# First gather one expert at a time, and a last expert with a plain one-hot, high and low parts, single blocks and a separate output buffer

## The chip, the cores and the metric

The kernel runs on one core of a Trainium2 chip. The metric is the time of one execution on the device in microseconds (us); shown are the median of several runs and one execution taken by the hardware profiler. TensorE is called PE (its weight loads PEld), VectorE V or DVE, ScalarE A or ACT, GpSimd G or POOL, and SyncE SP; SP issues the weight loads.

## The reference, cut to what matters

One transformer layer over 512 latent tokens with 1024 channels. The mixer (attention, Hyena, Fourier) comes first and isn't touched by the change. Then comes a mixture of 16 experts in which each expert chooses its 64 tokens, and a final norm:

```python
x = x + g1 * yx
h2 = modulate(rms_norm(x, norm2_g[l]), sh2, sc2)
x = x + g2 * expert_choice_moe(h2, w_router[l], w_gate[l], w_up[l], w_down[l])
return rms_norm(x, final_g)

def expert_choice_moe(h, w_router, w_gate, w_up, w_down):
    cap = CAPACITY_FACTOR * n // N_EXPERTS                  # 64
    aff = jax.nn.softmax(jnp.einsum('bld,de->ble', h, w_router), axis=-1)
    top_w, top_i = lax.top_k(aff.transpose(0, 2, 1), cap)
    xg = jax.vmap(lambda hb, ib: hb[ib])(h, top_i)
    a = jnp.einsum('becd,edf->becf', xg, w_gate)
    u = jnp.einsum('becd,edf->becf', xg, w_up)
    y = jnp.einsum('becf,efd->becd', jax.nn.silu(a) * u, w_down) * top_w[..., None]
    return scatter_add(y, top_i)                            # back to the tokens
```

Every expert has three weights of 8 MB in float32 (1024 x 2048 twice, 2048 x 1024), so 16 of them are some 400 MB that have to be read.

## The kernel before, in words

**The weights.** All expert weights form one stream of blocks of 1 MB (128 partitions x 2048 numbers): for each expert 8 blocks of wg, 8 of wu and 8 of wd. The last expert's wd is stored apart (`wdl`), in the order of the column blocks of `LASTD` (line 183): each entry has its first column, its width and how many of the 16 row blocks (fb) lie in each piece. `loads` (line 1101) gives the buffers in a fixed rotation: raw tiles that hold two blocks (T2b, T2a, T3a, T1_0, T1_1, wsp, T3b) and single `ld` buffers. The trace writes T1_0 and T1_1 both as rawT. `prefetch` (line 1116) issues the next load on SP's queue; where a raw tile takes the two halves of one pair of blocks, one load of 2 MB brings both (line 1129). SP's queue is in order: a load waits there until PE has read what was in the buffer. When the experts begin, 22 blocks have already been loaded.

**The gather.** Tokens are picked by matmul. `onehot` (line 1354) writes, for 128 tokens and one expert, which token goes to which of 64 places (`iota` equal to `slot`), times a value per token: rs4, the inverse norm, for the gather. `gather(pr)` (line 1362) does it for a pair of experts: eight one-hots, those of the second expert's last two token tiles on G, and then for each of 8 channel blocks k four matmuls into PSUM (gx), with x1 as weights and the one-hots of both experts as 128 moving columns. V and A move gx to xg with the norm's scale and shift. The pair's gather runs as a generator inside `up` of the expert ahead; for pair 0 it runs inside `up(0)` itself, one k ahead of each block of weights.

**An expert.** `up(e)` (line 1387) multiplies xg with wg (pa) and wu (pu), 4 matmuls of 512 columns a block, in pairs that fill the two halves of the array's columns; then silu, product (hid), transposition (hp, hidT). `down` (line 1431) multiplies with wd (py) and scales by g2b. `scatter_map` (line 1447) builds a one-hot with the affinity as value, transposes it (stp) to st, and after each pair 8 matmuls (sc) put the results back onto the tokens, where V adds them to acc. The order of the instructions on each engine is set by a scheduler, as far as data allow, from the order in which the code is written.

**The last expert** (lines 1491 to 1549). Its one-hot stands twice in st, because py keeps even and odd fb apart in two halves of the partitions and the scatter adds them. The columns are done in the four blocks of LASTD: py, V's multiply by g2b (Yq), four sc matmuls of full float32 in `finish` (line 1499), V's addition to x1, squares on A with their sums in ms16, and G's multiply of x1 by the final gain in place. `order` keeps PE's sequence of these as written; finish of a block comes after the first weight piece of the next. Then the mean of the squares, a root on A and a Newton step on V give r, x1 is scaled by it, and five stores write the output.

Of the kernel before, what the change touches and what calls it, by code (L numbers as in the profile page):

```python
# [182 lines left out]
LASTD = (0, 256, (8, 8)), (256, 256, (8, 8)), (512, 384, (4, 4, 4, 4)), (896, 128, (8, 8))  # L183
# [9 lines left out]
def _body(tc, nc, es, a, out, dbg, stop):  # L193
# [1253 lines left out]
    def scatter_map(pr, es2=(0, 1)):  # L1447

        for h_, e2 in enumerate(es2):
            onehot(oh, pr, e2, lambda t, e: aff[:, t, e:e + 1], h_)  # L1450
# [3 lines left out]
        st = M["mo"].tile([128, 512], F32, name="st")  # L1454
# [37 lines left out]
    st = scatter_map(7, (1, 1))  # L1492
# [3 lines left out]
    Yq = mo.tile([128, 1024], F32, name="Yq", tag="Y2")  # L1496
    order = tc.keep_in_program_order

    def finish(q):
# [15 lines left out]
        for t in range(0, 4, 2):  # L1515
            G.tensor_mul(x1[:, t:t + 2, qs], x1[:, t:t + 2, qs], fgb[:, None, qs].to_broadcast([128, 2, w]))
# [3 lines left out]
    for q, (c0, w, fbs) in enumerate(LASTD):  # L1520
# [11 lines left out]
        V.tensor_mul(Yq[:, qs], o[:, :w], M["g2b"][:, qs])  # L1532
    finish(len(LASTD) - 1)

    ms, s_, r = (mo.tile([128, 4], F32, name=n) for n in ("msf", "sf", "rf"))
    V.tensor_reduce(ms, ms16, axis=AX.X, op=OP.add)
    V.tensor_scalar(ms, ms, 1.0 / D, EPS, op0=OP.mult, op1=OP.add)
# [31 lines left out]
```

## Time and profile before

| what | us |
|---|---|
| median of three runs | 1476.78 |
| the three runs | 1473.26, 1477.72, 1476.78 |
| the profiled execution | 1474.33 |
| its span, first to last instruction | 1472.5 |
| PE busy, share of the span | 1354.8 (92%) |
| DVE, ACT, POOL busy | 495.1, 287.7, 114.8 |
| mean granted PE clock | 0.986 |

The profile's page says PE 48% and DMA 42% for the chain of work that ended last. Up to some 470 us the mixer runs; the route (norm, router, top 64) ends at 538 us; the experts take from there to 1464 us; scaling and storing the output take the rest. In the 40 slices of the page, DMA moves 382 to 396 GB/s from 552 to 663 us and 419 to 432 GB/s from there to 1436 us.

### The profile page before, as it was taken

What the parts mean: (1) busy time and instruction counts of PE and PEld (TensorE: products, weight loads), DVE (VectorE), ACT (ScalarE), POOL (GpSimd) and SP (SyncE); (2) the same over time, 40 slices, a digit from 0 to 9 for tenths busy, and PEclk for the clock granted to TensorE, in tenths of its full rate; (3) what the DMA queues carried; (4) which work ended last, traced back from release to release, by engine and by line L of the source; (5) the groups of instructions that cost most, each with busy time, mean ns of one, the idle gap of its engine ahead of it and who ended that gap; (6) DMA issues with size and microseconds to landing.
All of it is one profiled execution on the core that took longest, in us unless ns stands there. A gap on an engine that the chain in (4) does not pass through costs nothing.

```text
span 1472.5 us, 16253 instructions
## 1 busy us (share of the span) xinstructions
PE 1354.8 (92%) x6659; PEld 712.1 (48%) x6659; DVE 495.1 (34%) x984; ACT 287.7 (20%) x513; POOL 114.8 (8%) x141
## 2 busy tenths in 40 slices
PE   5899999999999989999999998988989988988996
PEld 2667668777788953433434333322423422423323
DVE  5676687665546551030121121120101101201123
ACT  5554225444334210000000000000000000000003
POOL 2133431000100100000000000000000000000002
PEclk9899999999999999999999999999999999999998
DMA  9424786111445489999999999999999999999994
GB/s 379 182 77 154 286 279 151 64 47 41 145 155 203 147 345 382 391 396 419 430 428 428 431 425 432 424 430 427 431 427 426 431 425 431 425 429 429 429 428 194
DMA packets 62037, 478.69 MB, mean 325 GB/s; under 512 B 6781, under 2 KB 11519, under 8 KB 17930
## 3 DMA queue, kind: packets, MB, share of 16 engines
q1 hardware_dynamic: 57384, 464.21, 76.9%
q0 software_dynamic: 2752, 9.05, 2.4%
q10 hardware_dynamic: 1826, 4.40, 0.9%
q8 instruction: 52, 0.85, 0.2%
q14 instruction: 23, 0.19, 0.0%
HBM read 473.02 MB, written 4.21 MB: 324 GB/s over the span
## 4 chain that ended last, share of the span: by engine, by line
PE 48%; DMA 42%; DVE 5%; ACT 3%; issue 1%; POOL 1%; ACTq 0%; SPq 0%; DVEq 0%
DMA rawwsp<-in_wu_dram 6%; PE pmm L229 6%; PE pmm L230 6%; PE pmm L231 6%; PE pa L1402 6%; PE pu L1402 5%; PE py L1438 5%; DMA ld<-in_wd_dram 4%; DMA rawT2b<-in_wu_dram 4%; DMA rawT<-in_wd_dram 3%; DMA rawT3a<-in_wd_dram 3%; DMA ld<-in_wg_dram 3%; DMA rawT<-in_wu_dram 3%; PE gx L1371 2%; DMA rawT2b<-in_wg_dram 2%; DMA ld<-in_wu_dram 2%
## 5 line engine op out<-in xcount | busy, mean ns | idle before, releaser
L1416 DVE TENSOR_TENSOR hid<-hid,pu 128x512 f32<-128x512 f32 x32 | 20.7, 684 | 419.8 <-PE pu L1402 406.2
L229 PE MATMUL pmm<-T,wsp 128*128 128x512 f32 x288 | 116.3, 407 | 0.7 <-ACT T L234 0.7
L231 PE MATMUL pmm<-T,wsp 128*128 128x512 f32 x288 | 113.9, 395 | 2.2 <-DVE wsp L235 2.2
L230 PE MATMUL pmm<-T,wsp 128*128 128x512 f32 x288 | 114.2, 397 | 0.1
L1415 ACT ACTIVATE hid<-pa 128x512 f32<-128x512 f32 x32 | 17.4, 594 | 408.1 <-PE pa L1402 390.2
L1371 PEld LDWEIGHTS gx<-vt,x 128*128 128x128 f32 x512 | 61.6, 191 | 41.3 <-issue 34.9
L1371 PE MATMUL gx<-vt,x 128*128 128x128 f32 x512 | 71.7, 287 | 4.5 <-DVE vt L1356 1.9
L1444 DVE TENSOR_TENSOR Y<-py,g2b 64x512 f32<-64x512 f32 x30 | 20.7, 689 | 161.8 <-PE py L1438 147.3
L1356 POOL TENSOR_SCALAR vt<-iota,slot,rs 128x64 f32<-128x64 f32 x16 | 10.3, 670 | 737.4 <-PE stp L1453 714.1
L235 DVE TENSOR_TENSOR wsp<-ld,wsp 128x1024 fp32r<-128x1024 f32 (+1 forms) x39 | 51.5, 1330 | 45.3 <-ACT wsp L234 43.1
L229 PEld LDWEIGHTS pmm<-T,wsp 128*128 128x128 f32 x288 | 54.4, 190 | 21.4 <-issue 7.8
L231 PEld LDWEIGHTS pmm<-T,wsp 128*128 128x128 f32 x288 | 54.6, 190 | 16.2 <-DVE wsp L235 2.6
L1480 PE MATMUL sc<-Y,st 128*128 128x512 f32 (+1 forms) x128 | 57.0, 598 | 4.8 <-DVE Y L1444 4.8
L230 PEld LDWEIGHTS pmm<-T,wsp 128*128 128x128 f32 x288 | 54.7, 190 | 12.6 <-issue 1.7
L1424 ACT ACTIVATE hidT<-hp 128x512 f32<-128x512 f32 x16 | 9.6, 598 | 249.1 <-PE hp L1419 129.6
L1438 PE MATMUL py<-rawT,hidT 128*64 128x512 f32 x216 | 50.0, 600 | 4.0 <-DMA rawT<-in_wd_dram 3.9
L234 ACT ACTIVATE wsp<-ld 128x1024 fp32r<-128x1024 f32 (+1 forms) x39 | 41.8, 1078 | 54.1 <-PE pmm L230 32.8
L1484 DVE TENSOR_TENSOR acc<-acc,sc 128x512 f32<-128x512 f32 x56 | 38.1, 686 | 12.3 <-PE sc L1480 12.3
L1480 PEld LDWEIGHTS sc<-Y,st 128*128 128x128 f32 (+1 forms) x128 | 23.5, 189 | 38.6 <-issue 26.4
L1402 PE MATMUL pu<-rawT,K1n 128*64 128x512 f32 x152 | 36.6, 599 | 3.3 <-DMA rawT<-in_wu_dram 3.2
L1438 PE MATMUL py<-ld,hidT 128*64 128x512 f32 x168 | 38.9, 596 | 0.5 <-DMA ld<-in_wd_dram 0.5
L1028 DVE TENSOR_REDUCE sm<-pbig 128x1 f32<-128x768 f32 x32 | 30.5, 955 | 17.2 <-PE pbig L1026 17.1
(566 smaller groups left out, 2337.3 us busy)
## 6 DMA issues: line engine op xcount, KB each, us to landing
ld<-in_wmod_dram SPq DMA_DIRECT2D x24, 1024.0 KB, 6.4
ld<-in_wg_dram SPq DMA_DIRECT2D x24, 1024.0 KB, 22.0
ld<-in_wd_dram SPq DMA_DIRECT2D x21, 1024.0 KB, 27.0
ld<-in_wu_dram SPq DMA_DIRECT2D x21, 1024.0 KB, 22.0
rawT<-in_wu_dram SPq DMA_DIRECT2D x10, 2048.0 KB, 9.2
ld<-in_win_dram SPq DMA_DIRECT2D x19, 1024.0 KB, 6.1
rawT<-in_wg_dram SPq DMA_DIRECT2D x8, 2048.0 KB, 29.2
rawT<-in_wd_dram SPq DMA_DIRECT2D x15, 1024.0 KB, 19.6
```

Source lines behind the costliest of these rows:

```text
L229: mm(o, ah, bh, start=first, stop=False)
L230: mm(o, ah, bl, start=False, stop=False)
L231: mm(o, al, bh, start=False, stop=last)
L234: keep(A.activation(hi, src, AF.Copy))
L235: keep((eng or V).tensor_sub(lo, src, hi.bitcast(F32)))
L1028: V.tensor_reduce(sm[:, 0:1], pb[:, :768], axis=AX.X, op=OP.max)
L1371: mm(o[:, k % 4], x1[:, t, k * 128:(k + 1) * 128], oh[:, t], start=t == 0, stop=t == 3)
L1402: mm(ob[64 * hf:64 * hf + 64], xg[:, k, es_], w_[:, (2 * b + hf) * 512:(2 * b + hf + 1) * 512], start=k == 0, stop=k == 7)
L1416: V.tensor_mul(hid[:, bs], hid[:, bs], acc_[1][b] if e == NE - 1 else acc_[1][:, bs])
L1438: mm(o[64 * dh:64 * dh + 64, :], hcol(hT_, fb), w_[:, i * 1024 + dh * 512:i * 1024 + (dh + 1) * 512], start=fb == 0, stop=fb == 15)
L1480: mm(o, st[ks, t * 128:(t + 1) * 128], Y2[ks, ds_], start=True, stop=True)
L1484: V.tensor_add(acc[:, t, ds_], acc[:, t, ds_], o)
```

## The change

Five things, all in the experts' part:

- `gather0` takes the place of gather(0): expert 0 first, with its four one-hots and 64 moving columns, then expert 1 with the same. Its generator has 16 steps instead of 8, and `up(0)` takes one ahead of each of its 16 blocks. G no longer writes one-hots.
- Two pairs of blocks in the last expert's wu (stream numbers 372 to 375) are loaded singly.
- The last expert's one-hot has no value; the affinity of its 64 tokens is gathered by 4 matmuls of one column (affc) and multiplied into Yq with g2b.
- LASTD's first two blocks of 256 columns become one of 512. For all blocks but the last, Yq is split into a high and a low part (A copies, V subtracts), and the scatter is two matmuls in the one-pass format per token tile instead of one in float32.
- The multiply by the final gain goes to a buffer of its own, xo, without waiting for the squares. V does it for two token tiles of the 384-wide block and for the whole last block. Part of the mean is taken ahead, two squares of the last block are on V, and the output leaves in seven pieces instead of five.

```diff
-LASTD = (0, 256, (8, 8)), (256, 256, (8, 8)), (512, 384, (4, 4, 4, 4)), (896, 128, (8, 8))
+LASTD = (0, 512, (4, 4, 4, 4)), (512, 384, (4, 4, 4, 4)), (896, 128, (8, 8))
...
-            if len(js) == 2 and stream[j][1] == 0:
+            if len(js) == 2 and stream[j][1] == 0 and j < 24 * NE - 12:
...
+    def gather0():
+        XG[0] = xg0
+        for h in range(2):
+            hs_ = slice(h * CAP, (h + 1) * CAP)
+            onehot(oh, 0, h, lambda t, e: rs4[:, t:t + 1], h)
+            for k in range(8):
+                if k % 4 == 0:
+                    o = pmm("gx")[:, :4 * CAP].rearrange("p (k n) -> p k n", k=4)
+                for t in range(4):
+                    mm(o[:, k % 4], x1[:, t, k * 128:(k + 1) * 128], oh[:, t, hs_], start=t == 0, stop=t == 3)
...
-            onehot(oh, pr, e2, lambda t, e: rs4[:, t:t + 1], e2, lambda t: G if e2 and t >= 2 else V)
+            onehot(oh, pr, e2, lambda t, e: rs4[:, t:t + 1], e2)
...
-        gat = gather(0) if e == 0 else gather(e // 2 + 1) if e % 2 and e < NE - 1 else iter(())
+        gat = gather0() if e == 0 else gather(e // 2 + 1) if e % 2 and e < NE - 1 else iter(())
...
-    st = scatter_map(7, (1, 1))
+    onehot(oh, 7, 1, None, 0)
+    onehot(oh, 7, 1, None, 1)
...
+        mm(o[:, :1], oh[:, t], aff[:, t, NE - 1:NE], start=t == 0, stop=t == 3)
+    affc, m0 = c16[:, 0:1], c16[:, 4:8]
+    V.tensor_copy(affc, o[:, :1])
...
-                order(mm(o[:, t - t0, :w], st[:, t * 128:(t + 1) * 128], Yq[:, qs], start=True, stop=True))
+                s_ = st[:, t * 128:(t + 1) * 128]
+                if q == last:
+                    order(mm(o[:, t - t0, :w], s_.bitcast(F32), Yq[:, qs], start=True, stop=True))
+                else:
+                    for i in range(2):
+                        order(mm(o[:, t - t0, :w], s_, Yhl[:, i, qs], start=i == 0, stop=i == 1))
...
-        for t in range(0, 4, 2):
-            G.tensor_mul(x1[:, t:t + 2, qs], x1[:, t:t + 2, qs], fgb[:, None, qs].to_broadcast([128, 2, w]))
+        if q < last:
+            for t in range(0, 4, 2):
+                (V if q == last - 1 and t else G).tensor_mul(xo[:, t:t + 2, qs], x1[:, t:t + 2, qs], fgb[:, None, qs].to_broadcast([128, 2, w]))
...
-        V.tensor_mul(Yq[:, qs], o[:, :w], M["g2b"][:, qs])
+        V.scalar_tensor_tensor(Yq[:, qs], o[:, :w], affc, M["g2b"][:, qs], op0=OP.mult, op1=OP.mult)
+        if q < last:
+            split(Yq[:, qs], Yhl[:, 0, qs], Yhl[:, 1, qs])
...
+    V.tensor_tensor(xo[:, :, qs], x1[:, :, qs], fgb[:, None, qs].to_broadcast([128, 4, qs.stop - qs.start]), op=OP.mult)
...
-    for i, (t, c0, c1) in enumerate(((0, 0, 512), (1, 0, 1024), (0, 512, 1024), (2, 0, 1024), (3, 0, 1024))):
+    for e_, t, c0, c1 in ((V, 0, 0, 512), (A, 1, 0, 512), (V, 0, 512, 1024), (A, 1, 512, 1024), (V, 2, 0, 1024), (A, 3, 0, 512),
+                          (V, 3, 512, 1024)):
```

What stands on PE in the first up projection, before, from the first gather matmul on (gx the gather, pa and pu the weights' matmuls, rawT_0 is T1_0; x7 are seven in a row, each of which the profile shows as two instructions):

```order
L1371 MATMUL gx<-vt,x_3183 128x128 x7
L1402 MATMUL pa<-rawT2b,K1n 64x512 x4
L1371 MATMUL gx<-vt,x_3183 128x128 x5
L1402 MATMUL pu<-rawT_0_4221,K1n 64x512
L1402 MATMUL pa<-rawT2b,K1n 64x512 x4
L1371 MATMUL gx<-vt,x_3183 128x128 x7
L1402 MATMUL pa<-rawT2a,K1n 64x512 x4
L1371 MATMUL gx<-vt,x_3183 128x128 x5
```

Two more groups of four follow among the later weights, six in all. Now, at the same place on PE:

```order
L1376 MATMUL gx<-vt,x_3183 128x64 x14
L1423 MATMUL pa<-rawT2b,K1n 64x512 x4
L1376 MATMUL gx<-vt,x_3183 128x64 x8
L1423 MATMUL pu<-rawT_0_4221,K1n 64x512
L1423 MATMUL pa<-rawT2b,K1n 64x512 x4
L1376 MATMUL gx<-vt,x_3183 128x64 x8
L1423 MATMUL pu<-rawT_0_4221,K1n 64x512
L1423 MATMUL pa<-rawT2a,K1n 64x512 x4
L1376 MATMUL gx<-vt,x_3183 128x64 x8
```

These hold all 32 matmuls of expert 0 and 6 of expert 1; the other 26 follow in seven groups of two or four between the pu blocks, eleven groups in all.

On PE behind the last up projection, before (py the down projection of the last expert, sc the scatter):

```order
L1528 MATMUL py<-rawT3b,hidT 64x256 x16
L1528 MATMUL py<-ld,hidT 64x256 x8
L1506 MATMUL sc<-Yq,st 128x256 x4
L1528 MATMUL py<-rawT2b,hidT 64x256 x8
L1528 MATMUL py<-rawT2b,hidT 64x384 x4
L1506 MATMUL sc<-Yq,st 128x256 x4
L1528 MATMUL py<-rawT2a,hidT 64x384 x8
L1528 MATMUL py<-ld,hidT 64x384 x4
L1528 MATMUL py<-ld,hidT 64x128 x8
L1506 MATMUL sc<-Yq,st 128x384 x4
L1528 MATMUL py<-rawT3a,hidT 64x128 x8
L1506 MATMUL sc<-Yq,st 128x128 x4
```

And now, where Yhl holds the high and low parts:

```order
L1570 MATMUL py<-rawT3b,hidT 64x512 x8
L1570 MATMUL py<-ld,hidT 64x512 x4
L1570 MATMUL py<-rawT2b,hidT 64x512 x4
L1570 MATMUL py<-rawT2b,hidT 64x384 x4
L1547 MATMUL sc<-Yhl,st_7364 128x512 x8
L1570 MATMUL py<-rawT2a,hidT 64x384 x8
L1570 MATMUL py<-ld,hidT 64x384 x4
L1570 MATMUL py<-ld,hidT 64x128 x8
L1547 MATMUL sc<-Yhl,st_7364 128x384 x8
L1570 MATMUL py<-rawT3a,hidT 64x128 x8
L1544 MATMUL sc<-Yq,st_7364 128x128 x4
```

Three scatters stand there instead of four, the first two with eight one-pass matmuls each.

V's queue, from the last block's Yq to the mean, now:

```order
L1578 SCALAR_TENSOR_TENSOR Yq<-py,c_81,g2b 128x128
L1558 TENSOR_TENSOR xo<-x_3183,K1n 128x2x384
L1549 TENSOR_TENSOR x_3183<-x_3183,sc 128x2x128
L1576 TENSOR_REDUCE c_81<-ms_7471 128x4
L1549 TENSOR_TENSOR x_3183<-x_3183,sc 128x2x128
L1577 TENSOR_SCALAR c_81<-c_81 128x4
L1552 SCALAR_TENSOR_TENSOR sqf,ms_7471<-x_3183 128x128
L1585 TENSOR_TENSOR xo<-x_3183,K1n 128x4x128
L1552 SCALAR_TENSOR_TENSOR sqf,ms_7471<-x_3183 128x128
L1583 SCALAR_TENSOR_TENSOR msf<-ms_7471,c_81 128x4
```

Before, only the two additions, one square and the two steps of the mean stood there.

## Rows read from the trace of the kernel before

**Rows 1.** Busy time by stretch: stretch, length, engines, PE clock, DMA share, GB/s.

```profile
560.00:660.00 100.00, 97.21 (x448) 37.74 (x448) 19.20 (x45) 6.99 (x13) 1.28 (x2) 1.00 0.99 403
660.00:664.00 4.00, 4.00 (x22) 1.31 (x20) 0.00 (x0) 0.00 (x0) 0.00 (x0) 1.00 0.75 221
664.00:1000.00 336.00, 317.42 (x1476) 119.70 (x1474) 50.80 (x108) 17.39 (x33) 3.84 (x6) 0.99 1.01 428
1000.00:1430.00 430.00, 385.91 (x1742) 140.14 (x1740) 65.39 (x133) 22.54 (x42) 3.84 (x6) 0.99 1.01 428
```

**Rows 2.** SP's DMA issues in order of time: start, duration, line, what.

```profile
649.25 0.33 SPq L1130 DMA_DIRECT2D rawT3a<-in_wu_dram  x1
660.74 0.33 SPq L1130 DMA_DIRECT2D rawT<-in_wd_dram  x1
...
1412.95 5.23 SPq L1134 DMA_DIRECT2D rawT2b<-in_wdl_dram  x2
...
1437.34 0.33 SPq L1134 DMA_DIRECT2D rawT3a<-in_wdl_dram  x1
```

**Rows 3.** PE's waits from 577 to 664: total us, times, longest.

```profile
PE pa L1402 <- ACT hid L1415: 1.8, 1, 1.8
```

**Rows 4.** PE's matmuls in order of time, start of the first up projection.

```profile
539.48 1.83 PE L1371 MATMUL gx<-vt,x 128*128 128x128 f32 x14 [1.88 <-DVE vt L1356]
541.24 1.94 PE L1402 MATMUL pa<-rawT2b,K1n 128*64 128x512 f32 x8
543.11 1.38 PE L1371 MATMUL gx<-vt,x 128*128 128x128 f32 x10
544.42 0.64 PE L1402 MATMUL pu<-rawT,K1n 128*64 128x512 f32 x1
```

**Rows 5.** PE's weight loads in order of time, for the router's 16-column matmuls.

```profile
483.93 0.98 PEld L1258 LDWEIGHTS lg<-wr,x1T 128*128 128x128 f32 x8
```

**Rows 6.** The chain that ended last, in order of time: start, us, what.

```profile
553.15 5.15 PE pa L1402 x24
```

**Rows 7.** V's instructions in order of time, the one-hots of pair 0.

```profile
538.22 1.43 DVE L1356 TENSOR_SCALAR vt<-iota,slot,rs 128x64 f32<-128x64 f32 x6
```

**Rows 8.** PE's matmuls in order of time, from the last up weights on.

```profile
1432.38 3.65 PE L1402 MATMUL pu<-rawwsp,xg 128*64 128x512 f32 x16 [1.21 <-DMA rawwsp<-in_wu_dram]
...
1457.50 1.09 PE L1528 MATMUL py<-rawT3a,hidT 128*64 128x128 f32 x16
```

**Rows 9.** DMA issues of the last down weights: count, KB, us from issue to landing.

```profile
rawT2b<-in_wdl_dram SPq DMA_DIRECT2D x1, 1024.0 KB, 29.2
...
rawT3a<-in_wdl_dram SPq DMA_DIRECT2D x1, 512.0 KB, 14.7
```

**Rows 10.** One-pass matmuls of 512 columns in the mixer, in order of time.

```profile
401.65 0.40 PE L229 MATMUL pmm<-T,wsp 128*128 128x512 f32 x1
401.89 0.39 PE L230 MATMUL pmm<-T,wsp 128*128 128x512 f32 x1
```

**Rows 11.** Groups by line and shape, V and A: count, busy us, mean ns, idle before.

```profile
L961 DVE SCALAR_TENSOR_TENSOR sg<-sg,pmm 128x512 f32<-128x512 f32 x16 | 11.0, 686 | 9.2 <-PE pmm L231 9.0
...
L378 DVE SCALAR_TENSOR_TENSOR E<-E,E 128x256 f32<-128x256 f32 x2 | 0.9, 426 | 0.1
...
L234 ACT ACTIVATE bh<-ld 128x512 fp32r<-128x512 f32 x16 | 10.0, 628 | 10.5 <-PE pmm L230 8.5 <-issue 1.2 <-DVE T2b L235 0.8
```

**Rows 12.** All engines in order of time, around the last additions and the mean.

```profile
1457.61 0.95 DVE L1508 TENSOR_TENSOR x<-x,sc 128x768 f32<-128x768 f32 x1 [0.33 <-PE sc L1506]
...
1458.71 4.98 POOL L1516 TENSOR_TENSOR x<-x,K1n 128x768 f32<-128x768 f32 x4 [4.35 <-ACT sqf L1514]
...
1460.19 0.75 DVE L1508 TENSOR_TENSOR x<-x,sc 128x256 f32<-128x256 f32 x2 [1.25 <-PE sc L1506]
...
1460.97 1.46 DVE L1511 SCALAR_TENSOR_TENSOR sqf<-x 128x128 f32<-128x128 f32 x1
...
1463.07 0.21 ACT L1538 ACTIVATE sf<-msf 128x4 f32<-128x4 f32 x1 [1.10 <-DVE msf L1537]
```

More of the change, by code (lines that the diff above doesn't have):

```diff
@@ L1352, in _body, with onehot @@
     XG = {}
-    def onehot(dst, pr, e2, val, h_, eng=None):
+    def onehot(dst, pr, e2, val, h_):
         for t in range(4):
-            (eng(t) if eng else V).tensor_scalar(dst[:, t, h_ * CAP:(h_ + 1) * CAP], iota, slot[:, t, 2 * pr + e2:2 * pr + e2 + 1],
-                            val(t, 2 * pr + e2), op0=OP.is_equal, op1=OP.mult)
+            d_, s_ = dst[:, t, h_ * CAP:(h_ + 1) * CAP], slot[:, t, 2 * pr + e2:2 * pr + e2 + 1]
+            if val is None:
+                V.tensor_scalar(d_, iota, s_, None, op0=OP.is_equal)
+            else:
+                V.tensor_scalar(d_, iota, s_, val(t, 2 * pr + e2), op0=OP.is_equal, op1=OP.mult)
     oh = flat(vt)[:, :512].rearrange("p (t n) -> p t n", t=4)
     xg0 = K1n[:, :1024].rearrange("p (k n) -> p k n", k=8)
+    def gather0():
[8 more added lines that the diff above has]
+                    mm(o[:, k % 4], x1[:, t, k * 128:(k + 1) * 128], oh[:, t, hs_], start=t == 0, stop=t == 3)
+                if k % 2:
+                    V.tensor_scalar(xg0[:, k, hs_], o[:, k % 4], A2[:, k:k + 1], S2[:, k:k + 1], op0=OP.mult, op1=OP.add)
+                else:
+                    A.activation(xg0[:, k, hs_], o[:, k % 4], AF.Identity, scale=A2[:, k:k + 1], bias=S2[:, k:k + 1])
+                yield
     def gather(pr):
@@ L1445, in down, with scatter_map @@
                          M["g2b"][64 * dh:64 * dh + 64, dh * 512:(dh + 1) * 512])
-    def scatter_map(pr, es2=(0, 1)):
-        for h_, e2 in enumerate(es2):
-            onehot(oh, pr, e2, lambda t, e: aff[:, t, e:e + 1], h_)
+    def scatter_map(pr):
+        for e2 in range(2):
+            onehot(oh, pr, e2, lambda t, e: aff[:, t, e:e + 1], e2)
         o = pmm("stp")
@@ L1453, in scatter_map @@
             T.transpose(o[:, t * 128:(t + 1) * 128], oh[:, t], ident)
-        st = M["mo"].tile([128, 512], F32, name="st")
+        st = M["mo"].tile([128, 512], F32, name="st", tag="st")
         A.activation(st, o, AF.Copy)
@@ L1491, in _body @@
     mo = M["mo"]
-    st = scatter_map(7, (1, 1))
+    onehot(oh, 7, 1, None, 0)
+    onehot(oh, 7, 1, None, 1)
+    o = pmm("stp")
+    for t in range(4):
+        T.transpose(o[:, t * 128:(t + 1) * 128], oh[:, t], ident)
+    st = mo.tile([128, 512], F32R, name="st1", tag="st")
+    A.activation(st, o, AF.Copy)
+    o = pmm("affc")
+    for t in range(4):
+        mm(o[:, :1], oh[:, t], aff[:, t, NE - 1:NE], start=t == 0, stop=t == 3)
+    affc, m0 = c16[:, 0:1], c16[:, 4:8]
+    V.tensor_copy(affc, o[:, :1])
     hT_ = up(15)
@@ L1496, in _body @@
     Yq = mo.tile([128, 1024], F32, name="Yq", tag="Y2")
+    xo = big1.tile([128, 4, 1024], F32, name="xo", tag="T1_1")
+    Yhl = big1.tile([128, 2, 2048], F32R, name="Yhl", tag="T1_0")
     order = tc.keep_in_program_order
+    last = len(LASTD) - 1
     def finish(q):
@@ L1509, in finish @@
         for t in range(4):
-            if q == len(LASTD) - 1 and t == 3:
+            if q == last and t > 1:
                 V.scalar_tensor_tensor(sq_[:, 512:512 + w], x1[:, t, qs], 1.0, x1[:, t, qs], op0=OP.mult, op1=OP.mult,
@@ L1531, in _body @@
                 finish(q - 1)
-        V.tensor_mul(Yq[:, qs], o[:, :w], M["g2b"][:, qs])
[L1533 to L1537, printed above, removed]
+        if q == last:
+            ms, s_, r = (mo.tile([128, 4], F32, name=n) for n in ("msf", "sf", "rf"))
+            V.tensor_reduce(m0, ms16[:, :, :last], axis=AX.X, op=OP.add)
+            V.tensor_scalar(m0, m0, 1.0 / D, EPS, op0=OP.mult, op1=OP.add)
+        V.scalar_tensor_tensor(Yq[:, qs], o[:, :w], affc, M["g2b"][:, qs], op0=OP.mult, op1=OP.mult)
+        if q < last:
+            split(Yq[:, qs], Yhl[:, 0, qs], Yhl[:, 1, qs])
+    finish(last)
+    V.scalar_tensor_tensor(ms, ms16[:, :, last], 1.0 / D, m0, op0=OP.mult, op1=OP.add)
     A.activation(s_, ms, AF.Sqrt)
+    V.tensor_tensor(xo[:, :, qs], x1[:, :, qs], fgb[:, None, qs].to_broadcast([128, 4, qs.stop - qs.start]), op=OP.mult)
     V.reciprocal(r, s_)
@@ L1548, in _body @@
             V.tensor_scalar(xv, xv, r[:, t:t + 1], None, op0=OP.mult)
-        (nc.scalar if t % 2 else nc.sync).dma_start(out[t * 128:(t + 1) * 128, c0:c1], xv)
+        (nc.scalar if e_ is A else nc.sync).dma_start(out[t * 128:(t + 1) * 128, c0:c1], xv)
 def kernel(**inputs):
```

5 lines of the change are left out of this document (3 added, 2 removed).

## The prediction

> **What bounds the kernel now.** I read the busy times by stretch first. From 664 us to 1430 us the DMA engines are busy all the time and move 428 GB/s; in the four us before that they have only 0.75 of it, and from 560 to 660 they have 403 GB/s [rows 1]. PE is busy nearly throughout both, so its busy share alone doesn't say who sets the end. The queue of loads does: at 660.74 the load into the raw tile T1_0 is issued 11.5 us after the one ahead of it [rows 2], because the buffer comes free only when PE has read it in the up projection of expert 2. The queue has run dry by then, and this is the last time. Behind that point the transfers run without a gap to the last expert, so whatever moves the issue at 660.74 moves the end by as much. Ahead of it PE runs in one chain from 539.48: its only longer wait in 577 to 664 us is 1.8 us for the ACT of the first expert [rows 3], and no load is waited for. So in this kernel a us of PE work in the first expert is a us of the whole, and a us of PE work between 664 and 1400 is nothing. The rest is the tail behind the last weights (1432.34 to the end).
>
> **The first gather, the largest term.** Before, 32 matmuls with 128 columns feed both experts of pair 0; the profile shows each as two instructions (x64 in all). The first 14 take 1.76 us from their start to the start of pa, the next 10 take 1.31 us [rows 4]: four more cost 0.45 us, so 0.112 us each and 0.20 us for entering and leaving the group. Now expert 0 and expert 1 get their own 32 matmuls with 64 columns: 128 instructions instead of 64. What one with 64 columns takes isn't in the trace, but both sides of it are: with 128 columns 0.112 us, and the router's matmul with 16 columns, on a full 128x128 weight load as here, 8 weight loads in 0.98 us, the last taking 0.19, so 0.79/7 = 0.113 us apart [rows 5]. Sixteen columns are no quicker than 128, so I take 0.112 for 64, with nothing to choose between the ends. The added 64 instructions are 64 x 0.112 = 7.1 us, and as the weights for gx (x1) have to be loaded again for each expert, none of it is hidden: PE has no idle time there.
>
> The Trainium skill states in "TensorE: Matmul & The Clock Gate", section "Back-to-back issue gap", that an isolated matmul's gap falls with its columns (N/2.4 ns and 2.5 ns more). By that rule the half-wide gather would cost no more than the whole one, and the sum below would be about -0.4 us instead of +6.7. The 16-column row speaks against it here; the case stands among the rivals.
>
> The order on PE also cuts the gather into more groups: 6 between weights before, 11 now. A group costs 0.20 us of its own, and the weight matmuls around it 0.15 more (8 of pa take 1.87 us beside a group, while 24 in a row take 5.15, so 8 take 1.72) [rows 4, 6]: 5 x 0.35 = 1.75 us. Single pu matmuls between the groups, which can't be paired, are as many as before.
>
> Against this, PE starts earlier. Before, its first matmul reads the one-hots of both experts and waits for the fifth of V's six, until 539.48; now it needs the first, 0.24 us long, which starts at 538.22 [rows 4, 7]: about 538.50, so 0.98 us gained. The next three one-hots come at 0.24 us each, which is the pace of two matmuls, so nothing more is lost. Sum: 7.1 + 1.75 - 0.98 = **+7.9 us** at the end of the first up projection (577 before, 585 now). I take +6 to +9 as its range.
>
> Does it reach the end? The down projection, expert 1 and its gather follow on PE in the same order as before, so the load issued at 660.74 goes out at about 668.6. Loads before it also come later, but none by more. The prefetched weights of expert 1 lie in SBUF long before, so PE waits for none. I put the whole 7.9 on the end.
>
> Later gathers lose POOL's two one-hots to V: eight of 0.24 us make 1.9 us instead of 1.43 [rows 7], while PE multiplies down weights for longer than that. Nothing, and if that cover were gone 0.5 us per pair.
>
> **The last weights.** The last two loads of up weights, 2 MB each, become four of 1 MB. PE waits now until 1432.34 for a whole pair, then has 16 matmuls of 3.65 us [rows 8]; half of them can be done before. hid, hp and py would start 1.7 us earlier. But the down blocks land one by one: the fourth, issued at 1412.95, at 1442.15, the last, issued at 1437.34, at 1452.04 [rows 2, 9]. The split doesn't move these, since the same bytes stand in the same queue. So py of the new 512-wide block ends not before 1442.15 and four matmuls of 0.43 us, which is 1443.9. The gain at hid is lost there.
>
> From there PE has 6.9 us of py (16 matmuls each of 384 and of 128 columns, at 0.43 us for 512), and two scatters of 8 one-pass matmuls. Such a matmul with 512 columns follows the one before it in 0.23 us (401.65 to 401.89) [rows 10]: 1.85 us, and 1.4 us with 384. New waits are in front of them: the multiply on V (0.69 us for 512), the high part on ACT (0.63), the low part on V (0.69, as the multiply) [rows 11], 2.0 us in all, while PE has 1.3 us of py to do, and so 0.75 us of waiting; in the second block about 1.5 us against 0.9, and with POOL then at work (below) I take 0.75 again. Nothing else can pass on PE, as its order is kept; behind it queue the remaining py blocks. With some 0.7 us for changes between shapes, py ends at 1443.9 + 6.9 + 3.25 + 1.5 + 0.7 = 1456.2, against 1457.50 + 1.09 = 1458.6 before [rows 8]: 2.4 us earlier.
>
> Part of that goes back on V. Its two adds of the 384-wide block, 0.95 us each [rows 12], the first from about 1454.9 when the first two tiles are scattered, end at about 1456.8 and stand ahead of the multiply for the last block, which starts at 1456.8 (before 1458.6): 1.8 left. The scatter of 128 columns is plain as before. Then V does the multiply by the final gain for two tiles of 384 ahead of its last adds, while POOL works on the other two. In the trace the square on V at 1460.97 takes 1.46 us where one of twice the width takes 0.43 [rows 11, 12], and it ends when POOL's first multiply does: V with two operands in SBUF stands still behind POOL. So I let that multiply wait for POOL, to 1458.6. Then come two adds (0.37 each) with the partial mean between them (0.5), two squares (0.4 each), between them the multiply for the last 512 elements (0.69), and the last step of the mean (0.2), some 3.3 us with the gaps: the root starts at about 1461.9, before at 1463.07 [rows 12]. Without the wait for POOL it would be 1461.4. **Tail: -1.2 us**, from -2.6 (nothing given back on V) to 0 (the split waits double).
>
> From the root on nothing is gained: the same Newton step, a first piece of the same 512 columns, and the same 2 MB to write, so seven stores instead of five give at most a few tenths either way.
>
> affc adds 4 small matmuls ahead of the last up projection, where PE waits for loads anyway; the one-hot without a multiply replaces one with.
>
> **Sum.** +7.9 - 1.2 = +6.7 us. The profiled execution took 1474.33 us (span 1472.5), so 1481.0 for one like it. The median of the three runs is 1476.78; with the profiled one the four have a mean of 1475.5. I take 1475.5 + 6.7 = **1482 us**.
>
> **Rivals.**
> - *Half the columns, half the time.* If a 64-column matmul takes half of 0.112 us, the added 7.1 us vanish: 7.9 - 7.1 - 1.2 = -0.4, so 1475. For it: where the columns are many they do set the pace, 512 in one pass 0.23 us apart [rows 10]. Against: 16 columns at 0.113 [rows 5]. It decides from below 0.094 us per instruction, where 128 of them bring the sum under 4.4 us. This one ends on the other side, not slower. Chance 0.07.
> - *The queue takes part of the delay.* If one of the 16 DMA engines lags behind its neighbours by 3 us and isn't idle at 661, that much of the shift only lets it catch up: +4.9 - 1.2 = +3.7, about 1479. For it: the share of the dry stretch is 0.75 and not near 0 [rows 1]. Against: the mean over four us can't tell one engine from another. Chance 0.12.
> - *The tail saves more.* If the waits for the split hide behind py and V has room, -3.5 us: +4.4, about 1480. Chance 0.06.
> - *The tail costs.* If V, with the splits and adds, is 1.6 us later than reckoned at both scatters, +2 instead of -1.2: +9.9, about 1485.4. Chance 0.05.
> - My forecast has 0.67, and what I haven't seen and what would make it faster 0.03.
>
> **How the numbers follow.** 0.3% of the time, 4.4 us, is about what a measurement of this kernel can tell from no change. Slower by more than that: most of the forecast (0.60 of 0.67), the costly tail (0.05) and half of the richer tail (0.03): 0.68. Same: the rest of these two, the cheap gather and the queue, 0.29. Faster: 0.03, as no case here comes to it. The range leaves out the cheap gather, the unseen and the far part of the costly tail: 1476 to 1486.
>
> **What would show it.** In the profile after: 128 gx instructions of 64 columns, 0.112 us apart, in the first up projection, and its end near 585; the load into T1_0 in expert 2 issued near 668 instead of 660.74, and 428 GB/s from 672 on; the last up weights landing near 1440; from that landing to the root about 29.5 us instead of 30.7. Wrong would be: gx 0.06 us apart; the first up projection ending at 577 or before; or the landing of the last up weights at 1432 although it ended later.

## The result and the profile after

| what | before | changed |
|---|---|---|
| median of eight runs each | 1474.66 | 1482.88 (1478.94 to 1486.13) |
| ratio, 95% interval | | 1.0055, 1.004 to 1.007 |
| predicted | | 1482.0 (1476.0 to 1486.0), slower by over 0.3% with 0.68 |
| the profiled execution, its span | 1474.33, 1472.5 | 1485.83, 1483.9 |
| all runs of this study, median (count) | 1474.42 (77) | 1479.58 (29) |

The change makes the kernel slower, by 8.2 us in the first eight runs, and over all runs of both by 5.2 us in the medians and 6.5 us in the means (predicted: 6.7). The difference of the two profiled executions, 11.5 us, is larger than either; why, these lines tell. First the busy time by stretch of the profile after (stretch, length, busy time of PE, PEld, DVE, ACT and POOL, PE clock, DMA share, GB/s), to be laid beside [rows 1]:

```profile
560.00:660.00 100.00, 97.20 (x484) 40.28 (x483) 12.89 (x36) 8.20 (x16) 0.00 (x0) 1.00 0.94 376
664.00:670.00 6.00, 6.00 (x19) 2.31 (x19) 4.35 (x7) 0.00 (x0) 0.00 (x0) 1.00 1.02 433
670.00:674.00 4.00, 4.00 (x22) 1.32 (x20) 0.00 (x0) 0.00 (x0) 0.00 (x0) 1.00 0.78 242
674.00:1000.00 326.00, 306.45 (x1430) 115.86 (x1428) 52.16 (x114) 17.38 (x33) 0.00 (x0) 1.00 1.01 428
...
540.00:546.00 6.00, 6.00 (x20) 3.04 (x19) 0.00 (x0) 0.58 (x2) 0.00 (x0) 0.50 0.35 139
...
1400.00:1406.00 6.00, 4.57 (x17) 1.34 (x13) 2.04 (x3) 0.00 (x0) 0.00 (x0) 1.00 1.06 449
1406.00:1423.00 17.00, 17.00 (x37) 7.37 (x37) 9.35 (x13) 0.60 (x1) 0.00 (x0) 0.52 1.01 428
```

The four us in which the DMA engines run dry stood at 660 to 664 before; they stand at 670 to 674 now, and from there the transfers move the same 428 GB/s. The last three rows are about what the profile of before does not have there: from 540 to 546 and from 1406 to 1423 PE was granted 0.50, the lower of its two levels (1.2 GHz). In the first case it had stood in gaps while the route ended and then worked without a break for 2.0 us, in the second it had been busy for 4.57 of 6 us and then without a break. Before, the second stretch had the full clock:

```profile
1406.00:1423.00 17.00, 15.75 (x74) 5.17 (x72) 1.21 (x2) 1.09 (x2) 0.00 (x0) 1.00 1.02 433
```

The queue of loads, whose issue at 660.74 set the end before [rows 2], in the profile after (start, duration, line, what):

```profile
659.02 0.33 SPq L1131 DMA_DIRECT2D rawT3a<-in_wu_dram  x1
670.51 3.76 SPq L1131 DMA_DIRECT2D rawT<-in_wd_dram  x2
```

9.77 us later than before, where 7.9 were forecast. And PE's first gather and last up weights, with the root (start, duration, engine, line, operands):

```profile
537.66 4.43 PE L1376 MATMUL gx<-vt,x 128*128 128x64 f32 x28 [0.99 <-DVE vt L1361]
542.02 3.68 PE L1423 MATMUL pa<-rawT2b,K1n 128*64 128x512 f32 x8
...
584.90 1.94 PE L1423 MATMUL pu<-rawmpart,K1n 128*64 128x512 f32 x8
...
1445.04 3.60 PE L1423 MATMUL pu<-rawwsp,xg 128*64 128x512 f32 x16
...
1473.97 0.20 ACT L1584 ACTIVATE sf<-msf 128x4 f32<-128x4 f32 x1 [0.92 <-DVE msf L1583]
```

The eight pa matmuls at 542.02 take 3.68 us, where the same eight take 1.94 at the full clock [rows 4]; the first up projection ends at 586.84 (before 577.1). The last row but one has no wait for a DMA: the last up weights had landed at 1441.70, but PE, slowed from 1406 to 1423, came to them five us later. So this execution shows the change and two stretches of half clock on top. The experiments take the two apart.

### The profile page after: what moved, and what is told of

It reads as the page before. It is cut to its first block, busy times and chain, and to the rows that moved or that the text cites. A ratio compares the mean times of both kernels' runs of the same rounds, so it can differ in the third digit from the quotient of the medians.

```text
span 1483.9 us, 16320 instructions
## 1 busy us (share of the span) xinstructions
PE 1368.2 (92%) x6691; PEld 720.0 (49%) x6691; DVE 501.2 (34%) x1010; ACT 288.4 (19%) x510; POOL 101.0 (7%) x120
## 4 chain that ended last, share of the span: by engine, by line
PE 52%; DMA 37%; DVE 5%; ACT 2%; issue 1%; POOL 1%; ACTq 0%; DVEq 0%; SPq 0%
PE pu L1423 7%; PE pa L1423 7%; PE py L1459 6%; PE pmm L229 6%; PE pmm L230 6%; PE pmm L231 6%; DMA rawT<-in_wg_dram 4%; DMA rawT2b<-in_wu_dram 4%; DMA rawT3a<-in_wu_dram 3%; DMA ld<-in_wd_dram 3%; DMA ld<-in_wu_dram 3%; DMA rawwsp<-in_wu_dram 2%; DMA rawwsp<-in_wd_dram 2%; DMA rawT3b<-in_wu_dram 2%; DMA ld<-in_wmod_dram 2%; DMA rawT3b<-in_wg_dram 2%
## 5 line engine op out<-in xcount | busy, mean ns | idle before, releaser
L1558 POOL TENSOR_TENSOR xo<-x,K1n 128x1024 f32<-128x1024 f32 (+1 forms) x3 | 6.5, 2192 | 950.3 <-DVE x L1549 950.3
L1392 PEld LDWEIGHTS gx<-vt,x 128*128 128x128 f32 x448 | 54.0, 191 | 35.2 <-issue 30.8
L1501 PE MATMUL sc<-Y,st 128*128 128x512 f32 (+1 forms) x128 | 61.5, 636 | 4.8 <-DVE Y L1465 4.8
L1392 PE MATMUL gx<-vt,x 128*128 128x128 f32 x448 | 63.0, 287 | 2.6 <-DVE K1n L1394 1.7
```

Source lines behind the costliest of these rows:

```text
L1392: mm(o[:, k % 4], x1[:, t, k * 128:(k + 1) * 128], oh[:, t], start=t == 0, stop=t == 3)
L1501: mm(o, st[ks, t * 128:(t + 1) * 128], Y2[ks, ds_], start=True, stop=True)
```

## The experiments

Two theories besides the prediction's were laid out: that the tail costs and the front costs less (B), and that the stretches of half clock are part of the change (C).

**The changed kernel again (e1).** No edit.

> The changed kernel once more, for a second profile of it. In its first profile PE had half the clock from 539.6 to 547 us and from 1406.7 to 1423 us; before had the full clock at both places. Theory A (prediction): the front costs about 7.9 and the tail gains 1.2 at the full clock; a profile without these two stretches should show a time near 1480 to 1481, the load into T1_0 of expert 2 issued 7 to 8 us later than before, and from the last landing to the end 1 us less than the 20.4 of before. Theory B (the tail costs): also without the stretches, the end lies 22 us or more behind the last landing, and the time is near 1484. Theory C (the clock is part of the change): both stretches are there again, at the same places.

Measured: 1479.40 us median of 12, ratio 1.0044 (1.0029 to 1.0059). Its profiled execution took 1478.81 and has the full clock at both places. PE's rows (first gather, first up projection, last expert), V's one-hots, V's and POOL's multiply by the final gain, SP's load, and the root:

```profile
536.30 1.88 DVE L1361 TENSOR_SCALAR vt<-iota,slot,rs 128x64 f32<-128x64 f32 x8
536.66 3.34 PE L1376 MATMUL gx<-vt,x 128*128 128x64 f32 x28 [0.99 <-DVE vt L1361]
539.93 1.94 PE L1423 MATMUL pa<-rawT2b,K1n 128*64 128x512 f32 x8
541.80 2.00 PE L1376 MATMUL gx<-vt,x 128*128 128x64 f32 x16
543.73 0.64 PE L1423 MATMUL pu<-rawT,K1n 128*64 128x512 f32 x1
...
562.67 1.11 PE L1376 MATMUL gx<-vt,x 128*128 128x64 f32 x8
563.70 1.94 PE L1423 MATMUL pu<-rawT,K1n 128*64 128x512 f32 x8
...
580.67 1.94 PE L1423 MATMUL pu<-rawmpart,K1n 128*64 128x512 f32 x8
...
666.28 3.76 SPq L1131 DMA_DIRECT2D rawT<-in_wd_dram  x2
...
1436.55 1.94 PE L1423 MATMUL pu<-rawwsp,xg 128*64 128x512 f32 x8 [0.52 <-DMA rawwsp<-in_wu_dram]
...
1446.74 3.42 PE L1570 MATMUL py<-rawT2b,hidT 128*64 128x512 f32 x16 [0.80 <-DMA rawT2b<-in_wdl_dram]
...
1450.92 1.91 PE L1547 MATMUL sc<-Yhl,st 128*128 128x512 f32 x7 [0.22 <-DVE Yhl L235]
...
1458.15 0.44 PE L1547 MATMUL sc<-Yhl,st 128*128 128x384 f32 x1 [0.43 <-ACT Yhl L234]
...
1460.17 1.09 PE L1570 MATMUL py<-rawT3a,hidT 128*64 128x128 f32 x16
...
1460.67 1.82 POOL L1558 TENSOR_TENSOR xo<-x,K1n 128x768 f32<-128x768 f32 x1 [2.69 <-DVE x L1549]
...
1461.58 1.74 DVE L1558 TENSOR_TENSOR xo<-x,K1n 128x768 f32<-128x768 f32 x1
...
1465.49 0.21 ACT L1584 ACTIVATE sf<-msf 128x4 f32<-128x4 f32 x1 [0.92 <-DVE msf L1583]
```

28 gx stand 3.27 us ahead of the weights behind them, 16 stand 1.93 and 8 stand 1.03: 0.112 us each and 0.14 for entering and leaving the group. V's first one-hot started at 536.30, so from there to the end of the first up projection (582.61) it is 46.31 us, before 38.87 (538.22 to 577.09, the end of the row below): +7.4.

```profile
573.07 4.02 PE L1402 MATMUL pu<-rawmpart,K1n 128*64 128x512 f32 x15
```

The start of the first one-hot itself differs by up to four us from profile to profile (535.5 to 539.6), with or without the change; all positions in the front are therefore taken from it. From the end of that projection to the load into T1_0 it is 83.67 us, before 83.65: the shift passes through whole. From the PE row that waits for the last up weights to the root it is 28.94 us, before 30.69. Behind the root 9.91 us are left to the end of the span, before 9.43, and 9.38 in e3 (below), whose code from there on is that of the changed kernel; no run shows why. Theory B is out: at the full clock the tail does not cost. C is out in its strict form, as the stretches need not come.

**The front alone (e2).** The kernel before, with gather0 of the change put ahead of gather, and

```
-        gat = gather(0) if e == 0 else gather(e // 2 + 1) if e % 2 and e < NE - 1 else iter(())
+        gat = gather0() if e == 0 else gather(e // 2 + 1) if e % 2 and e < NE - 1 else iter(())
```

> The kernel before with the first gather alone changed (one expert at a time, 64 columns). Theory A: +7 to +8 us against before. Theory B (the tail costs 2 us, the front less): about +6. Theory C: +5 at the full clock, more where PE has half the clock behind the start of the experts.

Measured: 1483.35, median of 6, ratio 1.0063 (1.0044 to 1.0082): +8.6 us on that chip's 1474.77. The profiled execution had a longer stretch of half clock than the changed kernel's:

```profile
540.00:553.00 13.00, 13.00 (x44) 7.29 (x44) 0.69 (x2) 0.75 (x3) 0.00 (x0) 0.51 0.18 74
```

The end of its first up projection and its load into T1_0:

```profile
588.38 1.94 PE L1419 MATMUL pu<-rawmpart,K1n 128*64 128x512 f32 x8
...
673.98 3.76 SPq L1130 DMA_DIRECT2D rawT<-in_wd_dram  x2
```

From first one-hot (537.46) to the end of the projection it took 52.86 us. In half-us stretches, 6.83 us of that were lost to the clock (half of the time at the lower level); 46.0 are left, +7.2 on before. The load into T1_0 goes out at 673.98, the same 83.66 us behind.

**The other parts alone (e3).** The changed kernel with the old gather for pair 0:

```
-        gat = gather0() if e == 0 else gather(e // 2 + 1) if e % 2 and e < NE - 1 else iter(())
+        gat = gather(0) if e == 0 else gather(e // 2 + 1) if e % 2 and e < NE - 1 else iter(())
```

> The changed kernel with the first gather as before, so the change's other parts alone (last expert's scatter, single blocks, final scale). Theory A: -1.2 us against before (-2.6 to 0). Theory B: +2. Theory C: near 0, and more in runs where PE has half the clock in the last two experts.

Measured: 1472.68, median of 12, ratio 0.9986 (0.9972 to 1.0001): -2.1 us, with an interval from -4.1 to +0.1. With e2 the two parts add up to +6.5, where the whole change gave +4.6 on the same chip (e1) and +8.2 in its first eight runs. PE's wait for the last up weights, its last py, and the root in the profile:

```profile
1434.61 1.94 PE L1406 MATMUL pu<-rawwsp,xg 128*64 128x512 f32 x8 [0.50 <-DMA rawwsp<-in_wu_dram]
...
1457.79 1.09 PE L1553 MATMUL py<-rawT3a,hidT 128*64 128x128 f32 x16
...
1463.12 0.21 ACT L1567 ACTIVATE sf<-msf 128x4 f32<-128x4 f32 x1 [0.92 <-DVE msf L1566]
```

28.51 us from the first to the last of them, 2.2 less than before.

**Twice the first gather (e4).** The changed kernel with

```
-                for t in range(4):
+                for t in (0, 1, 2, 3) * 2:
                     mm(o[:, k % 4], x1[:, t, k * 128:(k + 1) * 128], oh[:, t, hs_], start=t == 0, stop=t == 3)
```

> The changed kernel with every matmul of the first gather done twice (the first result is dropped): 128 more instructions of 64 columns in the first up projection. Theory A, one us of PE there is one us at the end, and 0.105 to 0.112 us for each whatever its columns: +13.4 to +14.3 us against the changed kernel, so some +21 to +22 against before. Rival (half the columns, half the time, 0.056 us each): +7 against the changed kernel. Rival (the queue of loads takes part of the delay): clearly less at the end than at the end of the first up projection.

Measured: 1494.14, median of 4, ratio 1.0142 (1.0118 to 1.0165): +19.4 us on before and 14.6 on the median of all runs of the changed kernel. A group of 26 in its profile, and the weights behind it:

```profile
549.62 3.12 PE L1376 MATMUL gx<-vt,x 128*128 128x64 f32 x26
552.67 1.94 PE L1423 MATMUL pa<-rawT2a,K1n 128*64 128x512 f32 x8
```

(3.05 - 0.14) / 26 = 0.112 us each. From first one-hot to the end of the projection 63.89 us, less 3.42 lost to the clock: 60.47, 14.2 above e1 for 128 instructions, 0.111 us each. Half the time for half the columns (+7) is out. From the end of the projection to the last landing of all loads it is 873.0 us here, 875.0 before and 873.8 to 874.8 in e1, e2 and e3. About one of these two us is PE's: its order differs here. The matmuls of expert 2 that read T1_0 stand ahead of the scatter, some of them in a wait for expert 1, so that the load into T1_0 goes out 75.4 us behind the projection instead of 83.65. The load into wsp, the next raw tile in the queue, shows what this saves PE. Before, and in e4:

```profile
667.61 0.33 SPq L1130 DMA_DIRECT2D rawwsp<-in_wd_dram  x1
688.88 0.33 SPq L1131 DMA_DIRECT2D rawwsp<-in_wd_dram  x1
```

It follows the projection by 90.52 us before and by 89.47 in e4. From it to the last landing it is 784.5 us before, 783.5 in e4, and 783.1 to 784.5 in all 14 profiles: the queue took none of the 14 us that could be told from this scatter.

**128 columns instead of 64 (e5 and e10, the same kernel).** Both experts' one-hots first, then every gx over all 128 columns, of which one half is dropped:

```
-                    mm(o[:, k % 4], x1[:, t, k * 128:(k + 1) * 128], oh[:, t, hs_], start=t == 0, stop=t == 3)
+                    mm(o[:, k % 4], x1[:, t, k * 128:(k + 1) * 128], oh[:, t], start=t == 0, stop=t == 3)
```

> The changed kernel, but each of the first gather's 128 instructions computes both experts' 128 columns (half of each result is dropped), with both experts' one-hots ahead of it. Theory A (a gx instruction takes 0.105 to 0.112 us whatever its columns): the gather's instructions stand as far apart as with 64 columns, PE starts about 1 us later behind the first one-hot, and the time is about 1 us above the changed kernel's 1480.7, so some +7 against before. Rival (a part of the time goes with the columns): over 0.112 us for each; at 0.02 us more, 2.6 us more at the end.

Measured: 1480.28, median of 6, ratio 1.0035 (1.0017 to 1.0053); in e10 (below) 1480.32, 1.0051 (1.0035 to 1.0066). The changed kernel had 1.0044 and 1.0035 on the same two chips. Groups of the profile, to be laid beside those of e1:

```profile
545.29 1.83 PE L1377 MATMUL gx<-vt,x 128*128 128x128 f32 x14
547.05 1.94 PE L1424 MATMUL pa<-rawT2b,K1n 128*64 128x512 f32 x8
...
559.60 1.16 PE L1377 MATMUL gx<-vt,x 128*128 128x128 f32 x8
560.69 1.07 PE L1424 MATMUL pu<-rawT,K1n 128*64 128x512 f32 x2
```

14 stand 1.76 us ahead of the weights and 8 stand 1.09: 0.112 us each, as with 64 columns, and 0.20 for the group instead of 0.14. So the halving of the columns gave back 0.06 us a group, and the gather's price is the number of its instructions. From first one-hot to the end of the projection it is 48.37 us without the lost time, 2.06 more than in e1: 0.90 from the later start of PE, and nearly all of the rest from two groups more and the 0.06. PE's order is that of e4 and saves 1.1 of it ahead of the load into wsp. The medians, 0.9 and 1.0 above those of the changed kernel, came out as expected, but as a sum of these, and not by the later start alone.

**Pairs again in the last up weights (e6).** As e3, with

```
-            if len(js) == 2 and stream[j][1] == 0 and j < 24 * NE - 12:
+            if len(js) == 2 and stream[j][1] == 0:
```

> As e3 (the change without its first gather), but the last up weights come in pairs of 2 MB again. Theory A (prediction: the earlier start of hid is lost to the landings of the down blocks): as e3, 1472.7, within 0.3 us; hid starts 1.7 us later, py of the 512-wide block ends at the same distance from the landings. Rival (the split is what the tail gains): 1.5 us slower than e3.

Measured: 1471.77, median of 12, ratio 0.9987 (0.9975 to 0.9999): no difference to e3 that can be told. PE's rows:

```profile
1430.67 3.65 PE L1406 MATMUL pu<-rawwsp,xg 128*64 128x512 f32 x16 [0.92 <-DMA rawwsp<-in_wu_dram]
1434.33 0.66 PE L1423 MATMUL hp<-packb,hid 128*128 128x128 f32 x4
...
1444.38 0.49 PE L1530 MATMUL sc<-Yhl,st 128*128 128x512 f32 x1 [0.23 <-ACT Yhl L234]
```

From the last up weights to hp it is 3.66 us here and 1.94 in e3 (1434.61 to 1436.55): the split gains 1.72 there, as forecast. At the first scatter it is 13.71 against 13.23, as PE in e3 has then waited twice for down blocks (0.38 and 0.42 us). 0.5 of the 1.7 is left.

**A plain scatter (e7).** As e3, without high and low parts:

```
-                if q == last:
-                    order(mm(o[:, t - t0, :w], s_.bitcast(F32), Yq[:, qs], start=True, stop=True))
-                else:
-                    for i in range(2):
-                        order(mm(o[:, t - t0, :w], s_, Yhl[:, i, qs], start=i == 0, stop=i == 1))
+                order(mm(o[:, t - t0, :w], s_.bitcast(F32), Yq[:, qs], start=True, stop=True))
...
-        if q < last:
-            split(Yq[:, qs], Yhl[:, 0, qs], Yhl[:, 1, qs])
```

> As e3, but the scatter stays float32 for all blocks: no high and low part, no copy on ACT, no subtraction on V. Prediction: PE needs 3.8 us instead of 1.85 for the 512-wide scatter (from 0.25 us for an instruction of 256 columns, 0.36 of 384) and 2.85 instead of 1.4 for the next, but waits 0.75 us less ahead of each: py ends 1.9 us later, and the time is 1.5 to 1.9 us above e3. Rival (V is what binds from there on, or the waits eat the gain): no difference to e3.

Measured: 1471.66, median of 12, ratio 0.9987 (0.9974 to 1.0001): none of the 1.5 to 1.9 us expected. In the profile the scatters cost what was expected:

```profile
1433.58 1.94 PE L1406 MATMUL pu<-rawwsp,xg 128*64 128x512 f32 x8 [0.49 <-DMA rawwsp<-in_wu_dram]
...
1446.71 3.70 PE L1525 MATMUL sc<-Yq,st 128*128 128x512 f32 x8
...
1455.23 2.85 PE L1525 MATMUL sc<-Yq,st 128*128 128x384 f32 x8
...
1463.02 0.20 ACT L1560 ACTIVATE sf<-msf 128x4 f32<-128x4 f32 x1 [0.92 <-DVE msf L1559]
```

3.70 and 2.85 us, but no wait ahead of them. From the last up weights to the root it is 29.44 us, 0.9 more than in e3. That is less than the runs here can tell: the split into parts is worth nothing by the runs and 0.9 of the tail's 2.2 us by the profile. With the 0.5 of e6, some 0.8 us would be left for the other parts (the buffer xo, the mean taken ahead, affc), which no run took apart.

**The old gather and a shorter way to the root (e8).** As e3, with the one-hots of pair 0 in order of token tile, and V's multiplies by the final gain moved: that of tiles 2 and 3 behind the first pieces of the output, that of the last block behind the mean.

```
+        for t_ in ((0,), (1,), (2,), (3,)) if pr == 0 else ((0, 1, 2, 3),):
+            for e2 in range(2):
+                onehot(oh, pr, e2, lambda t, e: rs4[:, t:t + 1], e2, t_)
...
-            for t in range(0, 4, 2):
-                (V if q == last - 1 and t else G).tensor_mul(xo[:, t:t + 2, qs], ...
+            for t in range(0, 2 if q == last - 1 else 4, 2):
+                G.tensor_mul(xo[:, t:t + 2, qs], ...
...
+        if (t, c0) == (2, 0):
+            qp = slice(LASTD[last - 1][0], qs.start)
+            order(V.tensor_mul(xo[:, 2:4, qp], x1[:, 2:4, qp], fgb[:, None, qp].to_broadcast([128, 2, qs.start - qp.start])))
```

> As e3, with two moves. The one-hots of the first pair in order of token tile, both experts' for a tile together, so that PE can start behind the second of eight instead of the fifth: 0.7 us earlier. And V's multiply by the final gain for tiles 2 and 3 of the 384-wide block (1.74 us in e3, of which 0.82 lie behind the end of POOL's own) goes behind the first pieces of the output, that of the last block behind the mean. Theory A (V stands still behind POOL, and that is on the path to the root): root 1.5 to 2 us nearer to the last landing than the 8.9 us of e3, time 2 to 2.7 us under e3, so 4 to 5 under before. Rival (the last additions wait for PE and not for V's multiply): 0.7 us under e3.

Measured: 1469.26, median of 12, ratio 0.9966 (0.9954 to 0.9978) to before: faster than both kernels, and 3.4 us under e3 in the medians. The profile explains about one of these:

```profile
1430.42 1.94 PE L1407 MATMUL pu<-rawwsp,xg 128*64 128x512 f32 x8 [0.50 <-DMA rawwsp<-in_wu_dram]
...
1456.37 0.42 DVE L1533 TENSOR_TENSOR x<-x,sc 128x256 f32<-128x256 f32 x1 [1.25 <-PE sc L1528]
...
1458.16 0.21 ACT L1568 ACTIVATE sf<-msf 128x4 f32<-128x4 f32 x1 [0.44 <-DVE msf L1567]
...
1460.37 0.95 DVE L1578 TENSOR_TENSOR xo<-x,K1n 128x768 f32<-128x768 f32 x1
```

27.74 us from the last up weights to the root, 0.8 less than e3: with V's multiply gone, the last additions wait for PE, as the rival had it. The multiply itself takes 0.95 us when POOL is at rest, 1.74 beside it (e1). In the front PE starts 0.59 us behind the first one-hot instead of 1.26, but the projection ends only 0.3 earlier (38.59 against 38.87), as PE then waits 0.33 us for ACT's first eviction. What the medians have beyond that no profile here shows. The means of the two variants lie 2.4 us apart, known to some 2 us, so chance can have made the rest.

**The clock (e9, e10, e11, e12).** The changed kernel a third time, e5 again, the kernel before (a profile alone) and e2 again (a profile alone).

> The changed kernel a third time, for the clock. Of five profiles with the first gather of before, PE lost 0, 1.7, 0, 1.7 and 0 us to stretches at half the clock in the first up projection; of five with the new one 3.4, 0, 6.8, 3.4 and 1.7. Theory C1 (the new gather itself brings the stretch): 3.4 us or more again, and a mean clock of the runs under that of before (0.9845 against 0.9856). Theory C2 (chance): a mean clock within 0.0005 of that of before.

> The variant with 128 columns (e5) a second time, since its PE starts 0.9 us later behind the route and its first six runs had a mean clock of 0.9860. C1: 1.7 us or more lost again, and a mean clock under that of before. C2: no difference to before. By the mechanism of e5, +6 against before at the same mean clock.

> The kernel before, for a second profile of it: C1: at most 1.7 us lost in the first up projection. C2: as often 3.4 or more as with the new gather.

> The first gather alone (e2), for a second profile: C1: 3.4 us or more lost in the first up projection. C2: none as often as with the gather of before. The first up projection, the lost time taken off, 46.1 us behind the first one-hot, as in e2.

Measured: e9 1479.35, median of 9, ratio 1.0035 (1.0021 to 1.0049), with a mean clock of its runs of 0.9866; e10 1480.32; e11 1473.55; e12 1483.09, its projection ending 47.94 us behind the first one-hot, 46.2 without the lost time, as in e2. The stretch of e9 behind the route:

```profile
540.00:543.00 3.00, 3.00 (x12) 1.77 (x13) 0.00 (x0) 0.40 (x1) 0.00 (x0) 0.50 0.58 246
```

Time lost to half clock in the first up projection, profile by profile: with the new gather 3.4, 0, 6.8, 3.4, 1.7, 1.7, 1.7 and 1.7 us (changed, e1, e2, e4, e5, e9, e10, e12), with the old one 0, 1.7, 0, 1.7, 0 and 0 (before, e3, e6, e7, e8, e11). That speaks for C1, though C1 was wrong in e9 and e12, where it asked for 3.4 us or more, and seven of eight against two of six can be chance. The mean clock of the runs speaks for C2: 0.9858 over the 69 runs of before in these experiments, 0.9851 over 29 of the changed kernel, 0.9866 in e9 alone. A line through all runs of all kernels, with one slope for all, gives some 0.82 us for each 0.001 of the mean clock; by it the difference of 0.0006 is half a us. But the mean clock is a weak witness, as it also holds the stretches at half clock between 664 and 1400 us, where the loads set the end. Whether the new gather brings such a stretch about, or only meets it, stays open: by the profiles it would be worth 2.0 us (2.6 lost on average against 0.6), by the mean clock half a us.

## Why the prediction was right, point by point

**Which chain sets the end.** Right. End of the first up projection to the load into T1_0: 83.65 us before, 83.66, 83.67 and 83.65 in e2, e1 and e3, while the projection's own end moved by up to 13 us. Behind the load into wsp the distance to the last landing stays within 1.4 us in all profiles, with the old gather and with the new. "I put the whole 7.9 on the end" holds, and the rival in which the queue takes part of the delay fell, by e4 too.

**The first gather.** +7.9 was forecast; 7.4 was measured in e1 at the full clock, 7.2 in e2 and 7.35 in e9 without the lost time. The bounds taken from the router's 16 columns and the old gather's 128 were the same number, and 64 columns gave it once more: 0.112 (e1, e4). PE starts 0.36 us behind the first one-hot instead of 1.26, a gain of 0.90 (forecast 0.98). The rest is 8.3 instead of 8.85, as a group of 64 columns costs 0.14 us of its own and not the 0.20 taken from the old gather.

The rule that spoke against it, a gap that falls with the moving columns (the Trainium skill, "TensorE: Matmul & The Clock Gate", section "Back-to-back issue gap"), does not govern this gather, by e4 and e5. In section "LDWEIGHTS (loading the stationary operand)" of that page, the Trainium skill puts the length of a weight load at the stationary matrix's columns over 1.2, in ns, an estimate of 107 ns for 128 columns; the 0.112 us of e1, e4 and e5 lie within 5% of it. That the load is what the spacing consists of is the reading that fits; no run here changed the load itself.

**The tail.** -1.2 was forecast, and -2.1 measured in e3, whose interval holds both. By the profiles the root lies 2.2 us nearer to the last up weights in e3 and 1.75 in e1; of these the changed kernel loses 0.5 behind the root, where a few tenths either way were forecast. Two steps were mis-sized. PE's waits for the parts were put at 0.75 us each; they are 0.03 + 0.22 and 0.43 + 0.15 in e1. That gain was lost again at the down blocks, for which PE waits 0.41 and 0.80, so that py ends 24.7 us behind the last up weights and not 23.9. Then V: from the end of py to the root 5.7 us were forecast and 4.2 came. That V's multiply has to wait for POOL was right: it ends 0.83 us behind POOL's end in e1, 0.82 in e3 and the first profile, 0.81 in e7, and takes 0.95 alone (e8). (The row of before that this was read from was misread: POOL's multiplies of 768 elements take 1.81 us each from 1458.71, so V's square, which ends at 1462.43, ends with the second of them and not with the first. That V waited for POOL there stands.) Too long was what follows: from V's multiply to the root 2.2 us, where 3.3 stood, since the short instructions on V overlap. The Trainium skill, "SBUF — State Buffer", section "SBUF: two separate sides", calls the port pair that V and GpSimd share an exclusive lock, held by whoever starts first for its whole instruction; these four ends agree with it.

"The gain at hid is lost there" was right but for 0.5 us (e6). The high and low parts matter less than reckoned (e7).

**The sum.** +7.4 - 2.1 = +5.3 by the parts at the full clock. The whole kernels agree: from first one-hot to the end of the span, lost time taken off, 939.1 and 939.6 us in e1 and e9, 934.3 and 933.7 before and in e11. e2 and e3 give +6.5 by their medians, all runs +5.2, the first eight +8.2. The forecast of +6.7 lies 1.4 above the sum of the parts at the full clock, 0.5 from the front and 0.9 from the tail; the half-clock stretches, for which the prediction has no term, can bring some of that back. That the first eight runs gave 1482.88 beside a forecast of 1482 is luck: all 29 have a median of 1479.58, and the 77 of before one of 1474.42 where the forecast started from 1475.5.

**What would show it.** The 128 instructions were there, the projection ended at 582.6 and 586.8 (585), the load went out at 666.28 and 670.51 (668), 428 GB/s followed, and the last up weights landed at 1436.5 and 1441.7 (1440), in e1 and in the first profile. Landing to root was 28.9 in e1 (29.5); in the first profile 32.3, as PE was late for them.

## What to carry to other kernels

In this kernel a small float32 matmul that needs its own weights costs by the instruction, not by its moving columns (0.112 us with 64 and with 128, 0.113 with 16): splitting one with 128 columns into two with 64 doubles its price. Before a piece is made ready earlier, look whether its cost lies on the chain behind which a saturated queue starts; there every us of it reaches the end. And a single profiled pair can differ by twice the effect: read the granted clock of each stretch first, and take positions from an event that the change doesn't touch.

## What the runs showed of the hardware

- PE was granted half its clock for stretches of some 3 to 17 us amid dense work, at places that differ from one execution to the next of the same kernel (1406 to 1423 us in one of three profiles of the changed kernel); others come back near one place, such as between 899 and 917 us in 11 of the 14 profiles. Where the end hangs on PE this is lost time: 3.4 us of the front in the first profile, and PE's late arrival at the last up weights.
- Eight matmuls of 64 columns and eight of 128 take 1.03 and 1.09 us to the next group (e1 and e5): the same 0.112 us each, and 0.06 more at the end of a group.
- V's multiply of 768 elements with both operands in SBUF takes 0.95 us alone and 1.74 beside POOL's; V's additions that read PSUM are not lengthened (1.82 for two, the second beside POOL, in e8; 0.95 each before).
